# A hybrid encoder layer on one core: operands of the matmuls begin at many byte offsets in one block of each projection

## The chip, the cores and the metric

The kernel runs on one NeuronCore of a Trainium2 chip. The time is device microseconds of one execution. Of the kernel before, three timed runs gave 2269.83 to 2270.15 us, with a median of 2270.11 us. The core's engines are TensorE (matmuls, PE in the profile, its weight loads PEld), VectorE (DVE), ScalarE (ACT), GpSimd (POOL) and SyncE (SP), which here issues nearly all transfers. A matmul multiplies a stationary operand, which a weight load brings into the array first, with a moving operand that streams past it column by column.

## What is computed

One layer of an encoder over 2048 prompt tokens and 8 x 16 sample tokens, model width 1024. It has four large projections, and the change touches three of them:

```python
qm, km, vm, om, ip, fp, qa, ka, va = split_in(x @ w_in)      # input projection
...
mix = jnp.concatenate([hm, ha], axis=-1) @ w_out             # output projection
h = layer_norm(DEEPNORM_ALPHA * x + mix, ln1_g, ln1_b)
f, conv_rows = conv_ffn(h, conv_prev, w_up, w_conv, b_conv, w_down)
y = layer_norm(DEEPNORM_ALPHA * h + f, ln2_g, ln2_b)
...
u = h @ w_up                                                 # up-projection, 1024 -> 5632
c = b_conv + sum(ext[:, j:j + T] * w_conv[j] for j in range(CONV_W))
a, g = jnp.split(c, 2, axis=-1)
return (jax.nn.silu(g) * a) @ w_down                         # down-projection, 2816 -> 1024
```

Between the first two stand a matrix-memory head group and a sliding-window attention group, whose small matmuls are woven into the large ones.

## The kernel before

**Arithmetic.** Every operand of a large matmul is split into two fp32r parts, hi (a cast by ScalarE) and lo (what the cast left, a subtraction by VectorE); this is `split`, lines 220 to 223. A product is then three matmuls: hi x hi, hi x lo, lo x hi. Each projection uses seven products for a two by two block multiplication instead of eight (a Strassen-like scheme); s = 1 to 7 names the product, and some products take sums or differences of weight quadrants. Such sums are made once, in block 0, written to DRAM, and loaded in later blocks (`SUMS`).

**Weight slots.** Split weights lie in slots of `WS` = 1088 columns of fp32, of which a weight unit uses 1024, so that it can begin up to 64 columns (256 bytes) into the slot. Eight slots (tags wlo, whi) and two more (wex) are used in turn. `half` (line 399) gives a slot to the input and output projections, `f_slot` (line 1787) to the up- and down-projection; both take the column `at` at which the unit begins.

**Input projection.** Four blocks of tokens (`IBLOCKS`), in each five groups g of output columns and seven products s. `next_split` (line 474) takes the next weight unit: it is split on the chip, or, if `kept` (line 428: block over 0, g from 2 on, s one of 6, 5, 7, 3), both halves are loaded ready-made from DRAM. It begins at column 16 for g below 2 and at column 48 for g from 2 on. `i_product` (line 714, matmuls at line 726) runs 24 matmuls of 256 columns for a product; for g below 2 the weights are the stationary operand and the tokens move, from g = 2 on it is the other way round. `i_direct` (line 740, matmuls at line 752) multiplies the gate and key-value weights with 264 columns.

**Up-projection.** Three blocks of tokens (`FBLOCKS`: 6, 6 and 5 tiles of 128), 22 column pairs j in each, seven products for each pair. `f_next` (line 1806) makes the weights of the next product, up to 6 products ahead of the matmuls in block 0 and 8 ahead after it: in block 0 all are split on the chip, and those of `SUMS` are also written to DRAM; in blocks 1 and 2 those of `SUMS` are loaded and three (s = 1, 2, 4) are split. They begin at column 48. `f_tokens` (line 1764) splits a quarter of a block's tokens into tiles of 4 x 384 columns, of which it uses the first h, 384 in blocks 0 and 1 and 320 in block 2. In `f_product` (line 1894, matmuls at line 1902) the weights are stationary and the tokens move, 12 matmuls for a product.

**Down-projection.** The same three blocks, seven products in six units of depth. `d_weights` (line 2036) loads and splits the weights of a unit into two slots, beginning at column 0; they are the moving operand, 512 columns, at line 2112. `d_tokens` (line 2054) splits the tokens, which are stationary.

In all three, TensorE runs its instructions in the order in which the program lists them; loads are issued by SyncE in order; the casts and subtractions stand in the orders of ScalarE and VectorE.

Other instructions that the working names: line 1366 transposes the attention's probabilities out of a tile whose rows are 2 x 128 + 4 = 260 columns apart; lines 1235, 1237 and 1244 multiply by v and by the memory C, whose heads are 129 columns apart, in plain fp32; line 1247 updates C head by head; line 1960 is two of the three taps of the causal convolution, which read `u[:, 1:]` and `u[:, 0:]`; line 1116 loads v (`v` in the rows) into heads 129 columns apart.

Of the kernel before, what the change touches and what calls it, by code (L numbers as in the profile page):

```python
# [206 lines left out]
class Prog:  # L207
# [265 lines left out]
    def next_split(self):  # L473
        V = self.nc.vector
        if self.us >= self.ur:
            return False
        u = self.uq[self.us]
        need = 1 if u[0] == "g" else 2
        if self.halves[0] - self.halves[1] + need > self.ring:
            return False  # L480
        self.us += 1
        if u[0] == "g":
            e = self.raw_of.pop(u)
            w = self.half(0, WS).rearrange("p (i k m) -> p i k m", i=2, k=2)[:, :, :, :264]
            self.split(w[:, 0], w[:, 1], e[0])
            e[1] = True
            self.wu[u] = w[:, 0], w[:, 1]
            return True
        at = 0 if u[0] == "o" else 16 if u[2] < 2 else 48
        hi, lo = self.half(at, 1024), self.half(at, 1024)  # L490
        if self.kept(u):
            for i, t in enumerate((hi, lo)):
                self.nc.sync.dma_start(t.bitcast(F32), self.zws[u[2]][SUMS.index(u[3])][i].rearrange("p a b -> p (a b)"))
        elif u[0] == "p" and u[1] == 0:
            self.split_first(u[2], u[3], hi, lo)
        else:
            e = self.raw_of.pop(u)
            self.split(hi, lo, e[0].rearrange("p a b -> p (a b)"))
            e[1] = True
        v = lambda t: t.rearrange("p (a b) -> p a b", a=2 if u[0] == "o" else 4)  # L500
        self.wu[u] = v(hi), v(lo)
        return True
# [491 lines left out]
    def one(self, n, sh, dt=F32):  # L994
        return self.tp.tile(sh, dt, name=n, tag=n, bufs=1)
# [698 lines left out]
    def f_setup(self):  # L1694
        nc, a, fp = self.nc, self.a, self.fp
        one = lambda n, sh, dt=F32: fp.tile(sh, dt, name=n, tag=n, bufs=1)
        self.cw = one("cw", [P, NUP, 4])
        nc.sync.dma_start(self.cw, a["cw"])

        nc.vector.tensor_scalar_mul(self.cw[:, :NFF], self.cw[:, :NFF], 0.5)  # L1700
        self.prev = one("prev", [P, 2, NFF, 2])
        nc.vector.memset(self.prev, 0.0)
        self.hraw, self.hc, self.wr, self.wc = {}, {}, {}, {}
        self.slot, self.made, self.u2 = -1, 0, {}
        nb = len(FBLOCKS)

        pairs = [(b, j) for b in range(nb) for j in range(NFF)]
        self.seq = [(0, 0, 1), (0, 0, 7)]
        for g in range(len(pairs)):
            self.seq += [(*pairs[g + d], s) for d, s in ORDER if 0 <= g + d < len(pairs)]  # L1710

        self.seq[-3:] = [(nb - 1, NFF - 1, s) for s in (5, 2, 3, 4)]
# [51 lines left out]
    def f_tokens(self, b, *steps):  # L1764

        V = self.nc.vector
        R, W = self.hraw[b], len(FBLOCKS[b]) * P
        h = W // 2
        r1, r2, r3, r4 = R[:, :4, :h], R[:, :4, h:W], R[:, 4:, :h], R[:, 4:, h:W]
        src = {1: r1, 7: r2, 6: r2, 2: r3, 5: r1, 3: r4, 4: r3}  # L1770
        for s in steps:
            if s == "t1":
                V.tensor_sub(r1, r2, r1)
            elif s == "t3":
                V.tensor_sub(r2, r4, r2)
            elif s == "t2":
                V.tensor_sub(r2, r4, r1)
            elif s == "t4":
                V.tensor_sub(r3, r3, r2)
            else:  # L1780
                pool = self.fp if s in (1, 7, 6) else self.f3 if s == 4 else self.f2
                hi = pool.tile([P, 4, 384], F32R, name=f"hh{s}", tag=f"hh{s}", bufs=1)
                lo = pool.tile([P, 4, 384], F32R, name=f"hl{s}", tag=f"hl{s}", bufs=1)
                self.split(hi[:, :, :h], lo[:, :, :h], src[s])
                self.hc[b, s] = hi[:, :, :h], lo[:, :, :h]

    def f_slot(self, at, dt=F32R):
        self.slot = (self.slot + 1) % 10
        if self.slot < 8:
            w = self.wp.tile([P, WS], dt, name="uw", tag=("whi", "wlo")[self.slot % 2], bufs=WB)  # L1790
        else:
            w = self.wx.tile([P, WS], dt, name="uw", tag="wex", bufs=2)
        return w[:, at:at + D].rearrange("p (k m) -> p k m", k=KD)

    def f_raw(self, b, j):

        nc = self.nc
        v, g = [self.wp.tile([P, KD, P], F32, name=n, tag="wraw", bufs=WR) for n in ("wv", "wg")]
        nc.sync.dma_start(v, self.a["wup"][j])
        if b == 0:  # L1800
            nc.sync.dma_start(g, self.a["wup"][NFF + j])
        else:
            nc.sync.dma_start(g[:, 4:], self.a["wup"][NFF + j][:, 4:])
        self.wr[b, j] = v, g

    def f_next(self):

        nc, V = self.nc, self.nc.vector
        if self.made >= len(self.seq):
            return False  # L1810
        b, j, s = self.seq[self.made]
        self.made += 1
        if s == 1:
            if (b, j) not in self.wr:
                self.f_raw(b, j)
            if b == 0:
                v, g = self.wr[b, j]
                s12, s34 = self.f_slot(48, F32), self.f_slot(48, F32)
                V.tensor_add(s12[:, :4], g[:, :4], g[:, 4:])
                V.tensor_sub(s34[:, :4], v[:, :4], g[:, :4])  # L1820
                V.tensor_sub(s12[:, 4:], s12[:, :4], v[:, :4])
                V.tensor_sub(s34[:, 4:], v[:, 4:], s12[:, 4:])
                self.wr[b, j] = v, g, s12, s34
        if s == 5 and (b, j) != (len(FBLOCKS) - 1, NFF - 1):
            self.f_raw(b + (j + 1) // NFF, (j + 1) % NFF)
        w = self.f_slot(48).rearrange("p (i k) m -> p i k m", i=2)
        i = SUMS.index(s) if s in SUMS else None
        keep = None if i is None else self.zw[j][i].rearrange("p (i k m) -> p i k m", i=2, k=4)
        if b and i is not None:
            nc.sync.dma_start(w.bitcast(F32), keep)  # L1830
        else:
            r = self.wr[b, j]
            q = {1: lambda: r[0][:, :4], 2: lambda: r[0][:, 4:], 4: lambda: r[1][:, 4:], 5: lambda: r[2][:, :4],
                 6: lambda: r[2][:, 4:], 7: lambda: r[3][:, :4], 3: lambda: r[3][:, 4:]}[s]()
            self.split(w[:, 0], w[:, 1], q)
            if i is not None:
                nc.sync.dma_start(keep, w.bitcast(F32))
        self.wc[b, j, s] = w[:, 0], w[:, 1]
        return True
# [196 lines left out]
    def d_weights(self):  # L2036

        if self.nw >= len(self.dseq):
            return
        b, s, u = self.dseq[self.nw]  # L2040
        self.nw += 1
        ks = DUNITS[u]
        m, k0, c0 = {1: (None, 0, 0), 2: (None, NK2, 0), 3: (None, NK2, 512), 5: (0, 0, 0), 7: (0, 0, 512), 4: (1, 0, 0), 6: (1, 0, 512)}[s]
        src = self.a["wdn"] if m is None else self.zt[m]
        src = src[k0 + ks[0]:k0 + ks[-1] + 1, :, c0:c0 + 512].rearrange("k p n -> p k n")
        n = len(ks) * 512
        raw = self.wp.tile([P, 1024], F32, name="wraw", tag="wraw", bufs=WR)
        hi, lo = [self.f_slot(0).rearrange("p a b -> p (a b)") for _ in range(2)]
        v = lambda t: t[:, :n].rearrange("p (a b) -> p a b", b=512)
        self.nc.sync.dma_start(v(raw), src)  # L2050
        self.low = self.split(hi[:, :n], lo[:, :n], raw[:, :n])
        self.dw[b, s, u] = v(hi), v(lo)
# [183 lines left out]
```

## Time and profile before

| | |
|---|---|
| median of 3 runs | 2270.11 us (2269.83 to 2270.15) |
| the profiled execution | 2270.08 us, span 2268.3 us |
| TensorE busy | 2251.2 us, 14293 matmuls |
| weight loads busy | 2081.9 us |
| VectorE, ScalarE busy | 1807.6 and 1273.1 us |
| transfers | 631.30 MB, mean 278 GB/s |

The profile is one execution. Its page gives busy times of the engines, the chain of work that ended last, and groups of instructions by line of the kernel. The trace behind it also answers by stretches of time (busy time and count of each engine), by line (least, median and greatest duration) and in the order of time. A matmul's duration in a row is the time from its start to its modelled end, so matmuls in a row overlap; their pace is read from starts, or from a stretch and its count.

### The profile page before, as it was taken

Reading aid. Unit: us, or ns where it says so; the run is one execution under the profiler, and the core shown is the slowest. Engines: PE = TensorE matmul, PEld = TensorE weight load, DVE = VectorE, ACT = ScalarE, POOL = GpSimd, SP = SyncE. Lnnn points to the kernel's source line nnn. Section 1 sums busy time; section 2 is a strip of 40 time slices with the busy share of each in tenths; the row PEclk is TensorE's granted clock in tenths of the full one; section 3 lists DMA queues with packets and bytes.
Section 4 is the critical chain, followed back from the end, with each engine's and each line's share of the span. In section 5 each row is a group of like instructions: output and inputs, shape, how many; then the busy total and the mean of one; then the engine's idle time right before and its main releaser. Section 6 shows DMA issues by size and latency. Waiting matters only on the chain.

```text
span 2268.3 us, 39783 instructions
## 1 busy us (share of the span) xinstructions
PE 2251.2 (99%) x14293; PEld 2081.9 (92%) x14293; DVE 1807.6 (80%) x3069; ACT 1273.1 (56%) x2374; POOL 270.3 (12%) x509
## 2 busy tenths in 40 slices
PE   9999999999999999999999999999999999999998
PEld 8999999999878778999999999999999988888887
DVE  9787687777698888998778777678766787896997
ACT  5453476776776656555656555556555644444452
POOL 0001001000021110211112000003211200100100
PEclk9999999999999999999999999999999999999999
DMA  8888998898997767898777999988998796757752
GB/s 304 315 314 317 317 320 275 277 315 294 331 325 262 275 216 282 305 330 302 279 284 261 308 307 311 314 274 277 316 304 263 253 318 207 255 188 234 247 171 89
DMA packets 302277, 631.30 MB, mean 278 GB/s; under 512 B 47420, under 2 KB 140672, under 8 KB 302080
## 3 DMA queue, kind: packets, MB, share of 16 engines
q1 hardware_dynamic: 296832, 614.01, 78.9%
q0 software_dynamic: 3520, 10.56, 1.5%
q10 hardware_dynamic: 1728, 4.20, 0.5%
q8 instruction: 113, 1.85, 0.3%
q14 instruction: 84, 0.69, 0.1%
HBM read 457.02 MB, written 171.64 MB: 277 GB/s over the span
## 4 chain that ended last, share of the span: by engine, by line
PE 80%; DVE 5%; issue 1%; ACT 1%; DMA 1%; POOL 0%; DVEq 0%; SPq 0%; ACTq 0%; POOLq 0%
PE dps L1902 20%; PE fup L1902 20%; PE dps L726 8%; PE fup L2112 7%; PE dps L2112 7%; PE fht L2112 5%; PE dps L227 2%; PE dps L228 2%; PE dps L229 2%; PE ppo L1372 1%; PE dps L752 1%; PE psc L1327 1%; PE ppt L1366 1%; DVE w L223 1%; PE fht L1724 1%
## 5 line engine op out<-in xcount | busy, mean ns | idle before, releaser
L1902 PE MATMUL fup<-hh,uw 128*128 128x384 f32 (+1 forms) x1848 | 476.8, 327 | 0.0
L1902 PE MATMUL dps<-hh,uw 128*128 128x384 f32 (+1 forms) x1848 | 476.7, 327 | 0.0
L1902 PEld LDWEIGHTS fup<-hh,uw 128*128 128x128 f32 x1848 | 329.6, 188 | 0.1
L1902 PEld LDWEIGHTS dps<-hh,uw 128*128 128x128 f32 x1848 | 329.5, 188 | 0.0
L1902 PE MATMUL fup<-hl,uw 128*128 128x384 f32 (+1 forms) x924 | 301.9, 327 | 1.2 <-DVE hl L223 1.2
L1902 PE MATMUL dps<-hl,uw 128*128 128x384 f32 (+1 forms) x924 | 301.7, 327 | 0.0
L1960 DVE SCALAR_TENSOR_TENSOR cc<-u,cw,cc 128x768 f32<-128x768 f32 (+1 forms) x264 | 258.1, 978 | 38.5 <-ACT cc L1958 32.1
L726 PE MATMUL dps<-w,oh 128*128 128x256 f32 x1344 | 251.2, 283 | 0.2 <-ACT dps L820 0.2
L222 ACT CAST uw<-wraw 128x1024 fp32r<-128x1024 f32 x126 | 123.9, 983 | 216.1 <-PE dps L2112 117.9
L223 DVE TENSOR_TENSOR w<-wraw,w 128x1024 fp32r<-128x1024 f32 (+2 forms) x163 | 186.5, 1150 | 63.8 <-ACT w L222 61.7
L222 ACT CAST w<-wraw 128x1024 fp32r<-128x1024 f32 (+2 forms) x163 | 160.7, 992 | 110.8 <-PE dps L726 55.4
L726 PEld LDWEIGHTS dps<-w,oh 128*128 128x128 f32 x1344 | 209.7, 188 | 11.3 <-issue 8.1
L726 PE MATMUL dps<-w,ol 128*128 128x256 f32 x672 | 187.1, 278 | 0.0
L223 DVE TENSOR_TENSOR uw<-wraw,uw 128x1024 fp32r<-128x1024 f32 x126 | 142.3, 1129 | 53.8 <-ACT uw L222 53.7
L1902 PEld LDWEIGHTS fup<-hl,uw 128*128 128x128 f32 x924 | 173.6, 188 | 1.9 <-DVE hl L223 1.8
L1902 PEld LDWEIGHTS dps<-hl,uw 128*128 128x128 f32 x924 | 173.6, 188 | 0.0
L726 PE MATMUL dps<-oh,w 128*128 128x256 f32 x896 | 167.4, 283 | 2.0 <-ACT mr L1177 0.9
L2112 PE MATMUL fup<-uw,fu 128*128 128x512 f32 x726 | 168.9, 389 | 0.0
L2112 PEld LDWEIGHTS fup<-uw,fu 128*128 128x128 f32 x726 | 136.3, 188 | 28.3
L2112 PE MATMUL dps<-uw,fu 128*128 128x512 f32 x660 | 160.7, 389 | 0.0
L2112 PEld LDWEIGHTS dps<-uw,fu 128*128 128x128 f32 x660 | 123.9, 188 | 25.8
L726 PEld LDWEIGHTS dps<-oh,w 128*128 128x128 f32 x896 | 139.8, 188 | 7.9 <-issue 4.1
(319 smaller groups left out, 4555.8 us busy)
## 6 DMA issues: line engine op xcount, KB each, us to landing
uw<-zw SPq DMA_DIRECT2D x176, 512.0 KB, 5.1
zw<-uw SPq DMA_DIRECT2D x88, 512.0 KB, 3.4
w<-zws SPq DMA_DIRECT2D x72, 512.0 KB, 5.9
wv<-wup SPq DMA_DIRECT2D x66, 512.0 KB, 5.3
wraw<-wi SPq DMA_DIRECT2D x65, 512.0 KB, 5.3
wraw<-zt SPq DMA_DIRECT2D x60, 512.0 KB, 3.8
wraw<-wdn SPq DMA_DIRECT2D x45, 512.0 KB, 3.9
wraw<-wo SPq DMA_DIRECT2D x40, 512.0 KB, 4.4
```

Source lines behind the costliest of these rows:

```text
L222: nc.scalar.copy(hi, src)
L223: return nc.vector.tensor_sub(lo, src, hi.bitcast(F32)).ins
L227: mm(out, ah, bh, start=start, stop=False)
L228: mm(out, ah, bl, start=False, stop=False)
L229: mm(out, al, bh, start=False, stop=stop)
L726: mm(o, l, r, start=s in (1, 7) and c == k == i == 0, stop=k == 3 and i == 2, skip_group_check=True)
L752: mm(o, x, w, start=k == i == 0, stop=k == KD - 1 and i == 2, skip_group_check=True)
L1327: nc.tensor.matmul(ps[kvh][:, j, :nk], q[rs, j0 + j], k[rs, sel], start=i == 0, stop=i == 2)
L1366: nc.tensor.transpose(pp[:, j * P:(j + 1) * P], scs[j // 2][:, 2 * kvh + j % 2, kt * P:(kt + 1) * P], self.ident)
L1902: mm(ps, l[:, k], r[:, k], start=s in (1, 7) and k == 0 and i == 0, stop=k == 3 and i == 2, skip_group_check=True)
L1960: V.scalar_tensor_tensor(c[:, v], u[:, i:i + n], w[i], c[:, v], op0=ALU.mult, op1=ALU.add)
L2112: mm(ps, l[:, k, c], r[:, k], start=s in (1, 4, 7) and u == 0 and k == 0 and i == 0, stop=u == nu - 1 and k == n - 1 and i == 2, skip_grou ...
```

## The change

In one block of each of the three projections the weight units begin at varying columns of their slots, and in block 2 of the up-projection the tokens begin at varying columns of their tiles. Columns are 4 bytes. Tiles and slots keep their sizes and places, and instructions keep their number and order.

- Input projection, block 1: a split unit begins at `2 * (13 * us % 32)`, that is at multiples of 8 bytes from 0 to 248; a loaded one at `4 * (5 * us % 16)`, multiples of 16 bytes from 0 to 240; `us` counts the units.
- Up-projection, block 1, and block 2 from j = 11 on: a split unit begins 27 columns further than the last, modulo 64 (steps of 4 bytes); a loaded one 20 columns further, modulo 64 (steps of 16 bytes). Elsewhere 48 as before.
- Up-projection, block 2: the tokens of product s begin at column 0, 1, 2, 4, 8, 12 or 16 for s = 1, 7, 6, 2, 5, 3, 4.
- Down-projection, block 1: both slots of a unit begin at `2 * (13 * nw % 32)`, multiples of 8 bytes; `nw` counts the units.

```diff
@@ next_split
         at = 0 if u[0] == "o" else 16 if u[2] < 2 else 48
+        if u[0] == "p" and u[1] == 1:
+            at = 4 * (5 * self.us % 16) if self.kept(u) else 2 * (13 * self.us % 32)
         hi, lo = self.half(at, 1024), self.half(at, 1024)
@@ f_setup
+        self.begins = [0, 0]
@@ f_tokens
-                self.split(hi[:, :, :h], lo[:, :, :h], src[s])
-                self.hc[b, s] = hi[:, :, :h], lo[:, :, :h]
+                at = {1: 0, 7: 1, 6: 2, 2: 4, 5: 8, 3: 12, 4: 16}[s] if b == 2 else 0
+                hi, lo = hi[:, :, at:at + h], lo[:, :, at:at + h]
+                self.split(hi, lo, src[s])
+                self.hc[b, s] = hi, lo
@@ new
+    def f_begin(self, b, j, i):
+
+        if b == 0 or b == 2 and j < 11:
+            return 48
+        if i is None:
+            self.begins[0] = (self.begins[0] + 27) % 64
+            return self.begins[0]
+        self.begins[1] = (self.begins[1] + 20) % 64
+        return self.begins[1]
@@ f_next
-        w = self.f_slot(48).rearrange("p (i k) m -> p i k m", i=2)
         i = SUMS.index(s) if s in SUMS else None
+        w = self.f_slot(self.f_begin(b, j, i)).rearrange("p (i k) m -> p i k m", i=2)
@@ d_weights
-        hi, lo = [self.f_slot(0).rearrange("p a b -> p (a b)") for _ in range(2)]
+        at = 2 * (13 * self.nw % 32) if b == 1 else 0
+        hi, lo = [self.f_slot(at).rearrange("p a b -> p (a b)") for _ in range(2)]
```

## The prediction

> **What bounds the kernel now.** I read the page first, then the waits of TensorE, then a table of busy time by stage, and last single groups of instructions.
>
> ```profile
> span 2268.3 us, 39783 instructions
> PE 2251.2 (99%) x14293; PEld 2081.9 (92%) x14293; DVE 1807.6 (80%) x3069; ACT 1273.1 (56%) x2374; POOL 270.3 (12%) x509
> PEclk9999999999999999999999999999999999999999
> DMA packets 302277, 631.30 MB, mean 278 GB/s; under 512 B 47420, under 2 KB 140672, under 8 KB 302080
> PE 80%; DVE 5%; issue 1%; ACT 1%; DMA 1%; POOL 0%; DVEq 0%; SPq 0%; ACTq 0%; POOLq 0%
> ```
>
> The waits of TensorE (who waited for whom, us in total, times, longest), its two largest:
>
> ```profile
> PE dps L337 <- DVE zero L332: 2.0, 1, 2.0
> PE ppt L1539 <- POOL v L1117: 1.4, 1, 1.4
> ```
>
> The reader is to see that TensorE is busy for 99% of the span, at the full granted clock, and makes up 80% of the chain that ended last; its waits for others are a few single ones. So the kernel's time is the number of matmuls times the pace of one, and the change, which removes and adds no instruction, can move the time in one of two ways: the pace of a matmul depends on where its operands start, or an engine or a transfer that feeds TensorE becomes so slow that TensorE waits.
>
> The stages that the change touches, cut at the first and last matmul of each block (columns: window, its length, busy time and instructions of each engine, granted clock, share of the DMA engines, GB/s): block 1 of the input projection, the up-projection's block 0, block 1 and two halves of block 2, and the down-projection's three blocks.
>
> ```profile
> 162.26:286.61 124.35, 122.98 (x1118) 117.04 (x1117) 86.62 (x168) 55.30 (x102) 15.30 (x14) 1.00 0.92 317
> 886.77:1213.42 326.65, 326.18 (x1898) 325.35 (x1897) 283.96 (x406) 194.70 (x325) 51.81 (x90) 1.00 0.80 295
> 1213.42:1538.54 325.12, 324.42 (x1889) 323.73 (x1889) 244.37 (x287) 175.86 (x275) 40.45 (x89) 1.00 0.89 296
> 1538.54:1674.72 136.18, 136.18 (x926) 136.17 (x925) 105.09 (x150) 73.52 (x138) 34.55 (x91) 1.00 0.92 310
> 1674.72:1810.40 135.68, 135.68 (x927) 135.68 (x926) 94.11 (x136) 75.45 (x141) 27.23 (x87) 1.00 0.84 262
> 1810.71:1967.99 157.28, 157.28 (x694) 129.91 (x693) 124.80 (x150) 72.61 (x90) 4.96 (x7) 1.00 0.76 262
> 1967.99:2125.26 157.27, 157.27 (x695) 129.92 (x694) 133.72 (x166) 71.35 (x87) 11.25 (x13) 1.00 0.66 218
> ```
>
> From these come the paces. The down-projection's block 1 has 693 matmuls of 512 columns (7 products, 11 slices of depth, 3 token groups, 3 terms): 157.27 / 693 = 226.9 ns. The second half of block 2 of the up-projection has 11 x 7 x 12 = 924 of 320 columns: 135.68 / 924 = 146.8 ns. The difference gives (226.9 - 146.8) / 192 = 0.417 ns a column, and 226.9 - 512 x 0.417 = 13.4 ns a matmul that doesn't depend on its width. At 384 columns that makes 173.5 ns. Block 1 of the up-projection (1848 of them) takes 325.12 / 1848 = 175.9 ns, its token transposes included.
>
> At 256 columns, in the input projection, two paces stand side by side in the order of time (start, length, instruction):
>
> ```profile
> 223.68 0.28 PE L726 MATMUL dps<-w,ol 128*128 128x256 f32 x1
> 226.51 0.28 PE L726 MATMUL dps<-w,ol 128*128 128x256 f32 x1
> 404.88 0.28 PE L726 MATMUL dps<-w,ol 128*128 128x256 f32 x1
> 405.90 0.28 PE L726 MATMUL dps<-w,ol 128*128 128x256 f32 x1
> 409.28 1.05 PE L1152 MATMUL pscore<-qk 128*128 128x128 f32 x8
> 410.17 0.60 PE L1162 MATMUL pkt<-ident,qk 128*128 128x128 f32 x4
> ```
>
> Between the first two rows lie 24 matmuls, 2.83 / 24 = 118 ns; between the next two lie 9, 1.02 / 9 = 113 ns. Eight passes of 128 columns took 0.89 us, 111 ns each, and each had its own weight load; so a weight load of 128 columns takes at most 111 ns. It is covered by 2 to 7 ns at 256 columns, by 36 ns at 320, by 62 ns at 384 and by 116 ns at 512.
>
> **The change part by part.** Where the starts move, counted from the code:
>
> - Input projection, block 1: 35 weight pairs. 23 are split on the chip (starts in steps of 8 bytes), 12 are loaded (steps of 16). For g below 2 the weights are stationary (14 products, 336 matmuls); for g from 2 on they are the moving operand (9 split and 12 loaded products, 216 and 288 matmuls).
> - Up-projection, block 1 and block 2 from j = 11: 99 split weight pairs in steps of 4 bytes (792 + 396 matmuls), 132 loaded ones in steps of 16 bytes. Weights are stationary here.
> - Up-projection, block 2: tokens, the moving operand, 264 matmuls for each product; s = 7, 6, 2, 5, 3, 4 start 4, 8, 16, 32, 48 and 64 bytes in, s = 1 stays.
> - Down-projection, block 1: 42 weight pairs, the moving operand of 693 matmuls, steps of 8 bytes.
>
> No instruction, tile or queue order changes: the last start is 62 of 64 spare columns in a weight slot, and 16 + 320 of 384 in a token tile.
>
> *Casts and subtractions.* They now write and read at starts off 8 and 16 bytes. What the trace has of that:
>
> ```profile
> L1960 DVE SCALAR_TENSOR_TENSOR cc<-u,cw,cc x87: 1009/1019/1022, 1221.4 to 1535.1; 128x768 f32<-128x768 f32 x87
> L1247 DVE SCALAR_TENSOR_TENSOR C<-C,wi,pcu x64: 322/342/351, 319.4 to 828.7; 128x129 f32<-128x129 f32 x64
> ```
>
> Columns are minimum, median and maximum in ns. Every second instruction of line 1960 reads at an odd word (u[:, 1:]), the others at an even one: all lie within 13 ns. Line 1247 reads and writes heads 129 words apart, so at all four words of 16 bytes: within 29 ns. I take 0 to 29 ns a split, and 0 for the time: VectorE is busy 244 of 325 us and 134 of 157 us in the stages concerned, behind TensorE's matmuls, and 42 splits of 29 ns are 1.2 us in the fuller one. Without that cover they would cost those 1.2 us there, 99 x 29 ns = 2.9 us in the up-projection and 0.7 us in the input projection. ScalarE (176 of 325 us) has more room.
>
> *Weight loads (stationary).* Nearest rows: the transposes of line 1366 take weights 260 words apart, so at all steps of 16 bytes within 64.
>
> ```profile
> L1366 PEld LDWEIGHTS ppt<-ident,sc x248: 137/141/144, 326.0 to 837.8; 128*128 128x128 f32 x124
> L1237 PE MATMUL pnum<-C,qk x120: 275/275/275, 348.7 to 827.0; 128*128 128x129 f32 x120
> L1244 PE MATMUL pcu<-v,kw x128: 272/275/277, 315.4 to 827.9; 128*128 128x129 f32 x128
> ```
>
> Within 7 ns: steps of 16 bytes are free. For 4 and 8 bytes there is no row; bounds are 0 and a load that takes twice as long (a rival below). A single extra piece of 16 bytes, 111 / 32 = 3.5 ns, vanishes behind 36 ns and more in the up-projection and costs at most 3.5 - 2 = 1.5 ns on half of 336 matmuls, 0.3 us. I take 0.3.
>
> *Moving operands.* Lines 1237 and 1244 stream operands that start at every word of 16 bytes (heads 129 words apart), and last the same to 5 ns. But these stream plain fp32, in two passes of half the rate (111 ns for 128 columns above, against 128 x 0.417 = 53); for fp32r at 0.417 ns a column every start in the trace is a multiple of 64 bytes. So the price is bounded: nothing from below; from above twice the column time. A stream read in pieces of 16 bytes, which is 4 columns, would cost one piece more for a start off 16 bytes: 1.67 ns. Such starts have 2 x 264 token matmuls, half of 693 and half of 216, together 983: 1.6 us. I take it, as the row nearest to this, the fp32 one, shows none or very little. Should the 13.4 ns between matmuls absorb it, the cost is nothing.
>
> [...]
>
> *Loads.* 24 transfers into the input weights and 132 into the up-projection's now land 16-byte steps off; issue, size and queue stay.
>
> ```profile
> uw<-zw SPq DMA_DIRECT2D x176, 512.0 KB, 5.1
> w<-zws SPq DMA_DIRECT2D x72, 512.0 KB, 5.9
> v<-zv SPq DMA_DIRECT2D x17, 256.0 KB, 6.5
> og<-zog SPq DMA_DIRECT2D x17, 256.0 KB, 5.5
> ```
>
> v lands in rows 516 bytes apart, so at starts of 4, 8 and 12 bytes, and takes 6.5 us against 5.5 for og: up to 18% longer, bounds 0 to 18%. The weights are asked for 8 products ahead, 8 x 12 x 147 ns = 14 us, so a landing 1 us later hides there. I take 0; without that lead each late landing would show as idle time of TensorE.
>
> **The sum.** The profiled execution took 2270.08 us (span 2268.3 and 1.8 around it), 0.03 from the median of 2270.11. 2270.1 + 0.3 + 1.6 = 2272.0 us; with the bounds of these terms alone 2270 to 2274.
>
> **The rivals.**
>
> *Larger pieces.* If the moving stream is read in pieces of 32 bytes, a start off them costs 8 x 0.417 = 3.3 ns. Such starts: 4 x 264 token matmuls, 3/4 of 693, 3/4 of 216 and half of 288, 1882 in all: 6.3 us, 2276.4. With pieces of 64 bytes it is 6.7 ns on 5 x 264 + 7/8 x 693 + 7/8 x 216 + 3/4 x 288 = 2331: 15.5 us, 2285.6. Against 64 bytes speaks the matmul of 264 columns, 16.5 pieces:
>
> ```profile
> 286.61 11.65 PE dps L752 x96
> ```
>
> 11.65 / 96 = 121.4 ns; 17 full pieces would be 272 x 0.417 + 13.4 = 126.8 ns. 32 bytes remain open. Chance 0.20, slower.
>
> *Halved rate.* If an operand off its granule costs two reads for each piece over its whole length, it decides from the first such start. Odd words alone: 264 matmuls of s = 7 gain 320 x 0.417 = 133 ns, 35 us; odd weight loads last 222 ns, 49 over the 173 ns of 396 matmuls and 75 over the 147 ns of 198, 34 us: 2339. With 16 bytes as the granule: 528 x 133 + 347 x 213 + 108 x 107 ns = 156 us, and loads 594 x 49 + 297 x 75 + 168 x 107 = 69 us: 2495. For it: full rate is not shown off 64 bytes. Against it: the fp32 rows above and VectorE's line 1960, where a contiguous stream shows nothing. Chance 0.14.
>
> *Transfers become the bound.* In block 1 of the up-projection the 88 loads are 46 of 96 MB, so 0.43 of the share of 0.89. From packets about a quarter longer the DMA engines are full and TensorE waits; twice as long gives 325 x 0.32 = 104 us there, by the same reckoning 52 in block 2 and 27 in the input projection: 2453. The 18% of v falls short of it. Chance 0.06. [...]
>
> *Faster.* If the two paces at 256 columns come from the starts, block 1's 840 matmuls could all fall to 113 ns: 840 x 4.6 = 3.9 us, 2266.2; more only if the 13.4 ns shrink as well. Against: both paces above come from products with the same start, 192 bytes past a multiple of 256. Chance 0.08, most of it counted as faster.
>
> **How the numbers follow.** Forecast 0.50, within 0.2% (4.5 us, about what a measurement of this kernel can tell from no change); remaining 0.02 for slower. Faster 0.07, same 0.51, slower 0.42. The range goes from 2266 (the faster rival) to 2290 (the larger pieces with some 4 us of late feeding) and leaves out 0.2 for the halved rate and the transfers.
>
> **What would show it.** The same windows: the down-projection's block 1 against block 0 (157.27 and 157.28 us now) shows the moving weights, block 2's halves (136.18 and 135.68) the tokens and, in the second, the weights; block 1 of the up-projection the stationary ones alone. A step of more than 2 us in one of them names the rival. A DMA share near 1.00 with idle TensorE names the transfers. If VectorE's splits grow by over 100 ns, the first step is wrong. The prediction fails if any window of these grows by over 1%.

## The result and the profile after

Five timed runs of the changed kernel gave 2278.86 to 2281.33 us, median 2279.27; five of the kernel before 2269.83 to 2270.73, median 2270.15. The ratio is 1.0043, with a 95% interval of 1.0028 to 1.0057: slower by 9.1 us. The profiled execution took 2281.05 us, 10.97 more than the profiled one before.

The page of the changed kernel, the lines that answer to those shown of before:

```profile
span 2279.3 us, 39783 instructions
PE 2260.4 (99%) x14293; PEld 2086.9 (92%) x14293; DVE 1808.0 (79%) x3069; ACT 1273.5 (56%) x2374; POOL 277.0 (12%) x509
PEclk9999999999999999999999999999999999999999
uw<-zw SPq DMA_DIRECT2D x176, 512.0 KB, 4.9
```

TensorE has the same 14293 matmuls at the same clock and is still busy for 99% of the span, but busy 9.2 us longer (2260.4 against 2251.2). So nearly all of the time went into matmuls, not into waiting for something else. The loads of the up-projection's kept weights take no longer (4.9 us against 5.1). VectorE's total is the same to 0.4 us, and the two convolution taps, now line 1975, again take at most 1022 ns.

Busy time by stage, cut at the matmuls at which the table of before is cut: block 1 of the input projection, block 1 and the two halves of block 2 of the up-projection, blocks 0 and 1 of the down-projection.

```profile
162.28:287.88 125.60, 124.22 (x1118) 118.26 (x1117) 86.81 (x168) 55.23 (x102) 14.93 (x14) 1.00 0.93 314
...
1215.13:1543.05 327.92, 327.24 (x1889) 326.57 (x1889) 244.49 (x287) 176.47 (x275) 40.40 (x89) 1.00 0.90 294
1543.05:1680.93 137.88, 137.12 (x926) 136.85 (x925) 105.09 (x150) 73.80 (x138) 33.60 (x91) 1.00 0.91 306
1680.93:1817.31 136.38, 136.38 (x927) 136.38 (x926) 94.29 (x136) 75.73 (x141) 27.34 (x88) 1.00 0.86 260
1817.60:1974.92 157.32, 157.32 (x695) 129.95 (x693) 124.31 (x149) 72.75 (x90) 6.75 (x5) 1.00 0.77 261
1974.92:2136.20 161.28, 161.28 (x694) 130.42 (x693) 134.59 (x167) 71.11 (x87) 15.52 (x13) 1.00 0.66 214
```

Against before, the stages grew by 1.25, 2.80, 1.70, 0.70, 0.04 and 4.01 us, 10.5 of the 10.97; the rest lies ahead of the up-projection, in stretches that differ by up to 2.3 us between kernels that have the same starts there (598.9 to 601.2 us, at the last experiment below). Each stage that the change touches grew; block 0 of the down-projection, which it doesn't touch, kept its time. The biggest item is block 1 of the down-projection: 4.01 us on 693 matmuls is 5.8 ns each. In the first half of block 2, 0.76 of the 1.70 us are idle time of TensorE: its list of waits has a single one of 0.8 us there, of line 1917 for ScalarE's line 1946. This wait isn't the change's doing: two experiments below that leave the up-projection alone, `down_pieces` and `down_tokens`, have it too (0.3 and 0.8 us).

What exactly became longer is seen in the groups of instructions of the down-projection's block 1: the matmuls and their weight loads before, in their own fence, then the same after. The last number but the idle time is the mean of one in ns.

```profile
L2112 PE MATMUL fup<-uw,fu 128*128 128x512 f32 x265 | 62.3, 389 | 0.0
L2112 PEld LDWEIGHTS fup<-uw,fu 128*128 128x128 f32 x265 | 49.7, 188 | 10.3
```

```profile
L2128 PE MATMUL fup<-uw,fu 128*128 128x512 f32 x264 | 63.7, 395 | 0.0
L2128 PEld LDWEIGHTS fup<-uw,fu 128*128 128x128 f32 x264 | 49.7, 188 | 11.8
```

The matmuls last 395 ns instead of 389, as their starts lie 5.8 ns further apart; the weight loads are recorded with 188 ns, as before. That figure alone proves little, since the loads of the up-projection are recorded with 187 to 188 ns too, where in block 2 a new matmul with its load starts every 147 ns. What speaks for a slower stream, and against a load that has become the longer of the two, are the widths below: where a start costs something, a matmul takes about 233 ns at 512 columns, 177 to 178 at 384 and 149 at 320. A load that set the pace would give the same figure at each width.

By start, this block suggests that the price doesn't follow how round the start is. Four units of 18 matmuls, whose weights begin 72, 32, 0 and 112 bytes into their slots:

```profile
1983.33:1987.57 4.24, 4.24 (x20) 3.40 (x18) 4.24 (x8) 1.78 (x2) 2.57 (x2) 1.00 0.85 300
2010.59:2014.79 4.20, 4.20 (x20) 3.37 (x18) 4.20 (x6) 1.82 (x3) 0.00 (x0) 1.00 0.51 153
...
2056.70:2060.79 4.09, 4.09 (x19) 3.38 (x18) 2.10 (x2) 1.78 (x2) 0.00 (x0) 1.00 1.03 342
2079.71:2083.79 4.08, 4.08 (x20) 3.38 (x18) 2.09 (x2) 1.78 (x2) 0.00 (x0) 1.00 0.57 172
```

Divided by 18, a matmul takes 235.6, 233.3, 227.2 and 226.7 ns. The multiple of 32 bytes costs nearly as much as the start at 72, and 112 bytes, no multiple of 32, costs nothing here. But 112 bytes aren't free by themselves: the same unit, with the same starts and after the same unit at 8 bytes, takes 4.15 / 18 = 230.6 ns a matmul in `only_down`, the first experiment below.

```profile
2071.66:2075.81 4.15, 4.15 (x19) 3.38 (x18) 2.10 (x2) 1.79 (x2) 0.00 (x0) 1.00 0.45 131
```

One start can thus settle at two paces, which limits what any single stretch below can prove.

### The profile page after: what moved, and what is told of

Same layout as the page of the kernel before. It is cut to its first block, busy times and chain, and to the rows that moved or that the text cites. A ratio compares the mean times of both kernels' runs of the same rounds, so it can differ in the third digit from the quotient of the medians.

```text
span 2279.3 us, 39783 instructions
## 1 busy us (share of the span) xinstructions
PE 2260.4 (99%) x14293; PEld 2086.9 (92%) x14293; DVE 1808.0 (79%) x3069; ACT 1273.5 (56%) x2374; POOL 277.0 (12%) x509
## 4 chain that ended last, share of the span: by engine, by line
PE 78%; DVE 6%; DMA 2%; ACT 2%; issue 1%; POOL 0%; SPq 0%; DVEq 0%; ACTq 0%; POOLq 0%
PE dps L1917 20%; PE fup L1917 20%; PE fup L2128 7%; PE dps L728 7%; PE dps L2128 7%; PE fht L2128 5%; PE dps L227 2%; PE dps L229 2%; PE dps L228 2%; DVE w L223 1%; PE ppo L1374 1%; PE psc L1329 1%; PE ppt L1368 1%; PE fht L1727 1%; PE dps L754 1%
```

## The experiments

Four theories are weighed in what follows. **Own start**: each stream is read in pieces of a fixed size, its granule, and a start off them costs something for each matmul, as the prediction had it. **Variation**: what costs is that the start changes from unit to unit. **Distance**: two streams run side by side, the moving operand and the next matmul's weights (in the down-projection's block 1 above, loads are recorded for 130.42 of the 161.28 us, in which matmuls are busy throughout), and what counts is how their two starts lie to each other. **Feeding**: late loads or splits. The trace above already spoke against the last.

### The parts add up: only_down, without_down

`only_down` has the change in the down-projection alone; `without_down` has all the rest of it.

```diff
# only_down: before, with
-        hi, lo = [self.f_slot(0)...
+        at = 2 * (13 * self.nw % 32) if b == 1 else 0
+        hi, lo = [self.f_slot(at)...
# without_down: the changed kernel, with these lines undone
```

> The down-projection's part of the change alone: weights of block 1 begin at multiples of 8 bytes. If the parts add, 2270.1 + 4.0 = 2274.2 us (the 693 matmuls of that block took 161.28 us in the changed kernel and 157.27 before), and all other stages as before. If the parts disturb each other through the feeding of TensorE, less than that here.

> The change without its down-projection part. If the parts add: 2269.8 + 1.3 (input projection) + 2.8 (up-projection, block 1) + 1.4 (block 2) = 2275.3 us, so that this and the down-projection alone (4.5 us over before) make 10.0, against 9.1 measured for all. If the feeding of TensorE decides, the parts do not add, and stray waits show in the list of TensorE's waits.

`only_down`: 2274.31 us against 2269.82 beside it, ratio 1.0020 (1.0011 to 1.0029). `without_down`: 2275.36 against 2270.25, ratio 1.0024 (1.0015 to 1.0034). 4.5 + 5.1 = 9.6 us, and the whole change costs 9.1: within these intervals the parts add. By stage, `only_down` (the input projection's block 1, and the down-projection's block 1):

```profile
162.01:285.79 123.78, 122.41 (x1118) 116.46 (x1117) 86.75 (x168) 55.36 (x102) 15.33 (x14) 1.00 0.94 321
...
1966.89:2128.20 161.31, 161.31 (x694) 130.42 (x693) 134.57 (x167) 71.17 (x87) 15.53 (x13) 1.00 0.65 213
```

`without_down` (the up-projection's block 1 and the two halves of block 2):

```profile
1214.10:1542.02 327.92, 327.24 (x1890) 326.58 (x1889) 244.45 (x287) 176.31 (x275) 40.24 (x89) 1.00 0.88 293
1542.02:1678.88 136.86, 136.86 (x927) 136.86 (x925) 105.37 (x150) 74.65 (x138) 34.08 (x91) 1.00 0.93 308
1678.88:1815.25 136.37, 136.37 (x927) 136.37 (x926) 94.28 (x136) 75.70 (x141) 27.26 (x88) 1.00 0.85 260
```

Block 1 of the down-projection costs the same 4.0 us alone, block 1 of the up-projection the same 2.80. Without the single wait the first half of block 2 grows by 0.68 us: this is the price of the moved tokens. One caution comes from the first row: the input projection's block 1 takes 123.78 us here with the starts of before, where the profile of before has 124.35. Seven of the profiles have that block unchanged; four take the longer time and three the shorter. Differences of half a microsecond in that block mean nothing, and its growth is 1.25 us or 1.8, by which of the two one compares with.

### A fixed start: up_const

Block 1 and 2 of the up-projection; weights (stationary) at a start that stays the same for five column pairs: 148, 160, 212, 216 and 192 bytes.

```diff
-        w = self.f_slot(48)...
+        at = (37, 40, 53, 54, 48)[min(j // 5, 4)] if b else 48
+        w = self.f_slot(at)...
```

> Kernel before, but in blocks 1 and 2 of the up-projection the weights begin at one fixed byte offset for five column pairs j each: 148 (j 0 to 4), 160 (5 to 9), 212 (10 to 14), 216 (15 to 19), then 192 as before. The tokens stay. Five j are 420 matmuls, 72.8 us at the 173.3 ns of 384 columns. Theory 'own start' (a weight load costs more when it begins off a multiple of 4, 8 or 16 bytes): 160 is the cheapest, like before; 148 and 212 (odd words) the dearest, 216 between. Theory 'distance' (the load of the next weights and the moving stream disturb each other, and the distance of their starts decides, aligned or not), with the single products of the changed kernel as its numbers: 148 and 216 like before (173.3 ns, 72.8 us), 160 about 178 ns (74.7 us), 212 about 179.7 ns (75.5 us). Theory 'variation' (only a start that differs from the unit before costs): all four like before.

2276.8 us. Stretches of 30 products that lie wholly within one start; first before (block 1 twice, the second stretch with 16 other matmuls in it, then block 2), then `up_const` (148, 160, 212 and 216 bytes in block 1, then the same four in block 2):

```profile
1220.64:1283.04 62.40, 62.40 (x362) 62.40 (x362) 49.30 (x59) 32.50 (x51) 7.08 (x20) 1.00 0.88 292
1366.24:1430.43 64.19, 64.19 (x378) 64.01 (x378) 46.74 (x57) 34.73 (x56) 5.55 (x18) 1.00 0.94 314
1667.68:1720.48 52.80, 52.80 (x362) 52.80 (x361) 35.68 (x53) 27.07 (x51) 8.30 (x34) 1.00 0.88 275
```

```profile
1221.40:1285.00 63.60, 63.60 (x362) 63.60 (x361) 49.28 (x59) 32.57 (x51) 7.11 (x20) 1.00 0.86 289
1295.61:1359.21 63.60, 63.60 (x361) 63.60 (x361) 46.67 (x57) 32.94 (x52) 5.63 (x18) 1.00 0.90 303
1369.93:1436.02 66.09, 66.09 (x378) 65.89 (x378) 46.64 (x57) 34.93 (x56) 5.70 (x18) 1.00 0.91 307
1447.45:1511.69 64.24, 64.24 (x378) 64.11 (x378) 46.62 (x56) 34.79 (x56) 5.91 (x18) 1.00 0.90 305
1550.25:1603.05 52.80, 52.80 (x361) 52.80 (x361) 42.35 (x60) 28.93 (x53) 14.77 (x37) 1.00 0.93 310
1611.85:1664.65 52.80, 52.80 (x363) 52.80 (x361) 39.59 (x58) 27.27 (x53) 9.60 (x34) 1.00 0.95 322
1673.51:1727.08 53.57, 53.57 (x362) 53.57 (x361) 35.80 (x53) 27.18 (x51) 8.30 (x34) 1.00 0.87 270
1735.84:1788.30 52.46, 52.46 (x362) 52.46 (x361) 35.66 (x53) 27.00 (x51) 8.30 (x34) 1.00 0.88 272
```

In block 1 (384 columns) 148 and 160 bytes both cost 1.20 us on 360 matmuls, 3.3 ns each; 212 bytes 1.90 on 376, 5.1 ns; 216 bytes nothing. In block 2 (320 columns) 148 and 160 cost nothing, 212 costs 0.77 / 360 = 2.1 ns, 216 gains 0.9 ns. So variation is out: a start that doesn't vary costs as well. A granule for the stationary operand's own start is out as well: an odd word (148) and a multiple of 32 bytes (160) cost the same in block 1 and 216 bytes nothing, and the same starts of 148 and 160 cost 3.3 ns in one block and nothing in the next. The two blocks differ in the width of the matmul and in what ran before; which of the two decides isn't shown.

### The moving operand, alone and with the stationary one: down_const, down_both

In the down-projection's block 0 the weights (moving) get one start for each product; in block 2, where each of the products s = 4, 6 and 7 has tokens of its own, the tokens (stationary) move along by the same distance, but for s = 7 of `down_const`, where the weights move alone.

```diff
# down_const (down_both has other numbers), d_weights and d_tokens
+        at = {0: {1: 28, 2: 18, 4: 30, 6: 16, 5: 32, 3: 48, 7: 1}, 2: {4: 18, 6: 30, 7: 18}}.get(b, {}).get(s, 0)
-        hi, lo = [self.f_slot(0)...
+        hi, lo = [self.f_slot(at)...
...
+        if b == 2 and s in (4, 6):
+            at = {4: 18, 6: 30}[s]
+            w = w[:, :, :, at:at + h]
# down_both
+        at = {0: {1: 64, 2: 4, 4: 8, 6: 2, 5: 60, 3: 56, 7: 44}, 2: {4: 16, 6: 8, 7: 4}}.get(b, {}).get(s, 0)
...
+        if b == 2 and s in (4, 6, 7):
+            at = {4: 16, 6: 8, 7: 4}[s]
+            w = w[:, :, :, at:at + h]
```

> Kernel before, but in the down-projection the weights of a whole product (99 matmuls of 512 columns, 22.4 us at 226.7 ns) begin at one fixed byte offset. Block 0, in the order of the products: s = 1: 112, 2: 72, 4: 120, 6: 64, 5: 128, 3: 192, 7: 4. Block 2 (66 matmuls for the products named): s = 4: weights and tokens both 72 bytes in, s = 6: both 120 in, s = 7: weights alone 72 in. Block 1 as before. 'Own start': 64, 128 and 192 are free (22.4 us), 112 too if 16 bytes are the granule, 72 and 120 cost about 0.7 to 0.8 us each, 4 at least as much; in block 2 both operands off 16 bytes cost at least as much a matmul as the weights alone. 'Distance': 112 free, 64 about +0.3 us, 128 about +0.5, 192 about +0.6, 72 +0.85, 120 +0.74, 4 unknown; in block 2 s = 4 and s = 6 are free (226.7 ns) and s = 7 costs 8 ns a matmul, 0.5 us. 'Variation': nothing costs, since the start stays through a product.

> Down-projection again, all else as before. Block 2, weights and tokens moved by the same amount: s = 4 by 64 bytes, s = 6 by 32, s = 7 by 16 (66 matmuls each, 226.7 ns before). Block 0, the weights alone, 99 matmuls each: s = 1: 256 bytes, 2: 16, 4: 32, 6: 8, 5: 240, 3: 224, 7: 176. Both streams at 72 and at 120 bytes cost 4.9 and 7.4 ns a matmul, the weights alone at 64 cost 6.6, so neither the distance alone nor the alignment alone tells the price. Theory 'distance in whole lines' (the two reads meet in the same part of the memory, which is laid out in lines; a common move by whole lines changes nothing): all common moves by at least one line are free, so 64 free if lines have at most 64 bytes, 32 too if at most 32, 16 too if at most 16; 72 and 120 aren't whole lines of 16. Theory 'own place' (each start counts for itself, modulo 256): common moves cost like the weights alone, 6.6 ns at 64. In block 0, by both theories 256 is free; by 'distance' the others cost 4 to 9 ns, aligned or not, and 16 and 32 no less than 8.

Before, a product of 99 matmuls in block 0, and 64 matmuls of a product in block 2:

```profile
1810.71:1833.15 22.44, 22.44 (x100) 18.58 (x99) 16.62 (x20) 11.02 (x15) 0.01 (x1) 1.00 0.91 288
2170.14:2184.64 14.50, 14.50 (x65) 12.01 (x64) 14.50 (x23) 7.41 (x10) 0.00 (x0) 1.00 0.44 133
```

`down_const`, 2275.05 us: weights alone at 112, 72, 64 and 4 bytes (99 matmuls), both operands at 72 and at 120, weights alone at 72 (64 matmuls):

```profile
1809.50:1832.38 22.88, 22.88 (x100) 18.56 (x99) 16.67 (x20) 11.06 (x15) 0.01 (x1) 1.00 0.91 297
1832.38:1855.67 23.29, 23.29 (x100) 18.70 (x99) 20.84 (x24) 11.33 (x16) 0.00 (x0) 1.00 1.02 394
1878.80:1901.90 23.10, 23.10 (x101) 18.71 (x99) 15.97 (x20) 9.98 (x12) 0.00 (x0) 1.00 0.66 219
...
1948.01:1971.52 23.51, 23.51 (x101) 18.72 (x100) 23.04 (x33) 10.04 (x13) 7.32 (x6) 1.00 0.76 264
2173.69:2188.51 14.82, 14.82 (x65) 12.11 (x64) 14.82 (x23) 7.42 (x10) 0.00 (x0) 1.00 0.41 128
2188.98:2203.96 14.98, 14.98 (x65) 12.08 (x64) 14.78 (x24) 10.40 (x18) 0.00 (x0) 1.00 0.69 221
2227.32:2242.39 15.07, 15.07 (x65) 12.08 (x64) 11.31 (x14) 8.82 (x11) 0.00 (x0) 1.00 0.16 52
```

`down_both`, 2273.06 us: weights alone at 256, 16 and 32 bytes (99 matmuls), both operands at 64, 32 and 16 (64 matmuls):

```profile
1809.11:1831.56 22.45, 22.45 (x100) 18.59 (x99) 16.64 (x20) 11.03 (x15) 0.02 (x1) 1.00 0.88 291
1831.56:1854.49 22.93, 22.93 (x100) 18.61 (x99) 20.57 (x24) 11.66 (x16) 0.00 (x0) 1.00 1.05 405
1854.49:1877.58 23.09, 23.09 (x101) 18.56 (x99) 22.72 (x28) 9.96 (x12) 0.00 (x0) 1.00 0.55 179
...
2172.41:2186.96 14.55, 14.55 (x66) 12.01 (x64) 14.55 (x23) 7.41 (x10) 0.00 (x0) 1.00 0.40 130
2187.42:2201.95 14.53, 14.53 (x65) 12.01 (x64) 14.53 (x23) 10.54 (x17) 0.00 (x0) 1.00 0.68 221
2225.72:2240.45 14.73, 14.73 (x66) 11.99 (x65) 11.31 (x14) 8.80 (x11) 0.00 (x0) 1.00 0.16 53
```

The pair that decides is 32 bytes: weights alone there take 23.09 / 99 = 233.2 ns a matmul, 6.6 more than at 0; with the tokens moved by 32 bytes too, 14.53 / 64 = 227.0, as good as free. The same with 64: alone 23.10 / 99 = 233.3, together 14.55 / 64 = 227.3. A start by itself is neither good nor bad; how the two streams lie to each other is what counts. Weights alone at 256 bytes are free again (226.8). At all the other starts that these two runs gave to the weights alone, round or not, the matmuls take longer, from 231.1 ns at 112 bytes to 237.5 at 4.

But the distance isn't all: moved together by 16, 72 and 120 bytes, matmuls take 230.2, 231.6 and 234.1 ns, 3.5 to 7.4 more, although the distance stays. All three are no multiples of 32. At 72 bytes the common move is still cheaper than that of the weights alone (231.6 against 15.07 / 64 = 235.5).

### How far it goes: down_pieces, down_tokens

`down_pieces` moves both operands in block 2, by 96, 48 and 8 bytes. `down_tokens` moves the tokens alone, by 192, 64 and 256 bytes.

```diff
# down_pieces, d_weights and d_tokens
+        at = {(2, 4): 24, (2, 6): 12, (2, 7): 2}.get((b, s), 0)
...
+        if b == 2 and s in (4, 6, 7):
+            at = {4: 24, 6: 12, 7: 2}[s]
+            w = w[:, :, :, at:at + h]
# down_tokens, d_tokens alone
+        if b == 2 and s in (4, 6, 7):
+            at = {4: 48, 6: 16, 7: 64}[s]
+            w = w[:, :, :, at:at + h]
```

> Block 2 of the down-projection, both operands moved by the same distance: 96 bytes (s = 4), 48 bytes (s = 6), 8 bytes (s = 7); 66 matmuls of 512 columns for each of the three products, 226.7 ns each before. Pieces of 32 bytes: 96 is free (under 0.8 ns), 48 and 8 cost 3 to 8 ns a matmul, 2270.5 to 2271.2 us in all. Pieces of 16 bytes: 96 and 48 are free, only 8 costs. The distance alone: all three are free. Every start that is no multiple of 64 bytes costs: 96 costs as well, 3 ns or more.

> Block 2 of the down-projection, the tokens (stationary) alone moved: 192 bytes (s = 4), 64 bytes (s = 6), 256 bytes (s = 7); the weights (moving) stay. If the distance of the two starts modulo 256 bytes decides, tokens at 192 stand as weights at 64 did (233.3 ns a matmul in block 0) and tokens at 64 as weights at 192 (233.4 ns), both 231 to 235 ns, and 256 is free (226.7): 2271 us in all. If only the moving operand's own start has a price, all three are free, 226.7 ns and 2270.2 us. If the order of the two matters, 192 and 64 differ by over 2 ns.

`down_pieces`, 2270.53 us (2271.28 beside it), 64 matmuls of each of the three products:

```profile
2169.80:2184.35 14.55, 14.55 (x66) 12.01 (x64) 14.55 (x23) 7.39 (x10) 0.00 (x0) 1.00 0.45 139
2184.81:2199.73 14.92, 14.92 (x65) 12.03 (x64) 14.71 (x24) 10.32 (x18) 0.00 (x0) 1.00 0.69 207
2223.08:2237.90 14.82, 14.82 (x65) 12.10 (x64) 11.29 (x14) 8.79 (x11) 0.00 (x0) 1.00 0.15 53
```

96 bytes: 227.3 ns, free. 48: 233.1, 8: 231.6. So a common move is free at 32, 64 and 96 bytes and costs at 8, 16, 48, 72 and 120: pieces of 32 bytes fit all eight, pieces of 16 fail on 16 and 48. Each of the eight is one stretch of one run.

`down_tokens`, 2271.82 us:

```profile
2171.35:2185.99 14.64, 14.64 (x65) 12.02 (x64) 14.56 (x23) 7.41 (x10) 0.00 (x0) 1.00 0.48 144
2186.45:2201.39 14.94, 14.94 (x66) 12.03 (x65) 14.72 (x24) 10.32 (x18) 0.00 (x0) 1.00 0.65 203
2224.73:2239.24 14.51, 14.51 (x65) 12.01 (x64) 11.29 (x14) 8.79 (x11) 0.00 (x0) 1.00 0.16 54
```

Tokens alone at 64 bytes take 233.4 ns and at 256 nothing extra (226.7), as the distance has it: moving the stationary operand slows the stream just as moving the streamed one does. Yet 192 bytes take 228.8, where 231 to 235 was expected because weights at 64 took 233.3. A distance taken modulo 256 bytes is therefore too simple to give the price. Whether the two directions differ, or this is another case of one relation that settles at two paces, one stretch doesn't tell.

### Can starts be chosen to gain: in_const, starts_chosen

In the input projection `in_const` gives each block one start for stationary and one for moving weights; `starts_chosen` then takes those that looked best, and 216 bytes in the up-projection's block 2.

```diff
# in_const
+        if u[0] == "p":
+            at = ((12, 16), (22, 28), (56, 8), (0, 40))[u[1]][u[2] > 1]
# starts_chosen
-        at = 0 if u[0] == "o" else 16 if u[2] < 2 else 48
+        at = 0 if u[0] == "o" else 22 if u[2] < 2 else 28
...
-        w = self.f_slot(48)...
+        w = self.f_slot(54 if b == 2 else 48)...
```

> Kernel before, but in the input projection the weights begin at one fixed byte offset in each block (g below 2, where they are stationary; g from 2 on, where they move): block 0: 48 and 64, block 1: 88 and 112, block 2: 224 and 32, block 3: 0 and 160 (before: 64 and 192 everywhere). It asks whether the two paces of 256 columns, 113 and 118 ns, follow the distance of the two starts. 'Distance': whole blocks sit at one pace, and 88 (113.5 ns in one product of the changed kernel) and 112 (115 to 117) are the fast ones; the best case for block 1 is 3 us less than before. 'Own start': 64, 32, 160, 0 and 224 alike, 88 slower. If the paces come from interruptions by other matmuls, all blocks show both, as before, and the time stays within 2 us of 2270.

> A version with starts chosen from these traces: input projection at 88 bytes for g below 2 and 112 for g from 2 on in every block (block 1 of the run with fixed starts had 75 and 81% of its matmuls at the fast pace, against 37 and 21% before), up-projection block 2 at 216 bytes (145.7 ns against 146.7 there). If the two paces follow the starts: 336 x 1.8 + 504 x 2.6 ns in block 1, about half of that each in blocks 2 and 3, so 3.7 us, and 1848 x 1.0 ns = 1.8 us: 5.5 us below the kernel before, about 2264.4. If the paces of the input projection come from interruptions: only the 1.8 us, 2268.

`in_const` took 2272.3 us. Its block 1 (starts at 88 and 112 bytes), and all that follows up to the up-projection (blocks 2 and 3 with 224, 32, 0 and 160 bytes):

```profile
162.72:285.50 122.78, 121.08 (x1118) 115.16 (x1117) 86.41 (x168) 55.23 (x102) 15.32 (x14) 1.00 0.94 324
285.46:887.95 602.49, 600.64 (x4253) 520.23 (x4251) 477.27 (x1232) 409.48 (x1010) 76.61 (x103) 1.00 0.85 288
```

The second stretch takes 600.20 us before (286.57 to 886.77), so these blocks seemed to lose 2.3 us, while block 1 seemed to gain 1.0 to 1.6. But kernels that leave the input projection alone take from 598.9 (`down_both`) to 601.2 us (`down_tokens`) for the second stretch, so the loss is 1.3 to 3.6 us by the kernel one compares with, and whether the two paces of 256 columns follow the starts stays open. `starts_chosen` was to turn that into a gain: 2268.96 us against 2270.25, ratio 0.9995 (0.9986 to 1.0004), which can't be told from no change. The input projection's block 1 took 123.11 us against 123.78 and 124.35 with the old starts, and the second half of the up-projection's block 2 this:

```profile
1673.81:1809.50 135.69, 135.69 (x927) 135.69 (x926) 94.14 (x136) 75.56 (x141) 27.34 (x87) 1.00 0.84 262
```

That is 135.68 before: the 0.9 ns a matmul that 216 bytes had gained there in `up_const` didn't come again. The expectation of 2264.4 failed; the 2268 of its other theory is met only in number, since the 1.8 us on which it rested, from 216 bytes, aren't there. With that went the hope that a table of good starts can be read from one run.

## Why the prediction was right or wrong

The direction was right and the time lay inside the range, but the forecast of 2272.0 was 7.3 us short: the sum gave the change 1.9 us, and it costs 9.1. The forecast of "within 0.2%" failed with it, and so did the prediction by its own sign: no window was to grow by over 1%, and the down-projection's block 1 grew by 2.5%. That the time lies in the range is luck, for its upper end came from 32-byte pieces priced stream by stream and from 4 us of late feeding, and neither is what happened.

- **What bounds the kernel** held. TensorE's busy time grew by 9.2 us, and the stages of the tables carry the whole difference: 1.25 + 2.80 + 0.68 + 0.70 + 4.01 = 9.4 us.
- **Casts and subtractions at no cost** held: VectorE's total is 1808.0 us against 1807.6.
- **Loads at no cost** held: 4.9 us to landing against 5.1 in the up-projection, DMA share 0.90 against 0.89 in its block 1, and no wait of TensorE for a load in its list. The input projection's loads took 6.3 us against 5.9, inside the bound of 18% and without a wait.
- **Weight loads (stationary), 0.3 us**: this step failed. In the up-projection's block 1 they are the only thing moved, and it grew by 2.80 us. The prediction took the danger to be a longer load, and hid it behind 36 ns of cover. The recorded loads didn't get longer (188 ns); the matmuls streaming beside them did. Cover for the load says nothing about that. `down_tokens` shows it alone: with only the stationary operand moved 64 bytes, a matmul takes 233.4 ns instead of 226.7, at 512 columns, where the prediction saw 116 ns of cover.
- **Moving operands, 1.6 us**: the term was mis-sized, and the step behind it (a start off 16 bytes costs one piece more) was wrong. Half of the down-projection's 693 matmuls were to pay 1.67 ns each, 0.6 us; the block grew by 4.01. Unit by unit in the changed kernel, all starts but 0, 112 and 64 bytes pay 3.9 ns or more, multiples of 16 among them, and 64 pays 3.1. The tokens' share came out close to its term by another road: 0.68 us in the first half of block 2, where the prediction had 0.44 (264 starts off 16 bytes). No run shows pieces of 16 bytes, from which this term and the 0.3 us were built: moved together by 16 and 48 bytes the operands cost 3.5 and 6.4 ns a matmul at 512 columns (`down_both`, `down_pieces`). The fp32 rows on which the small price rested show no effect of their starts (272 to 277 ns for 129 columns); the fp32r matmuls do (395 ns against 389 in the down-projection's block 1). (The last start in a weight slot is column 63, reached in the up-projection, and not 62; it still fits, and nothing hangs on it.)
- **The rivals.** The larger pieces saw something: 32 bytes is a size that the runs show (common moves of 32, 64 and 96 bytes took 227.0 to 227.3 ns a matmul). But the rival priced each stream by its own start, 3.3 ns off a piece and nothing on it, and weights alone at 32 bytes cost 6.6 ns. Its 2276.4 us is nearer to the result than the forecast, by a reckoning that isn't the one at work. The halved rate is out (no start cost more than 11 ns a matmul), the transfers too (DMA share 0.90 in the up-projection's block 1, no wait for a load). The faster one needed starts that help: `starts_chosen` looked for them and found no gain that can be measured.

What the prediction lacked is a rival in which two streams that are each fine alone disturb each other. The evidence within reach was that in the kernel before every pair of fp32r streams starts at multiples of 64 bytes, so that its rows could show neither the common nor the single move.

**What stays open.** That two reads at the same time share some part of the memory is argued from the pace, which depends on both starts (233.2 ns for weights alone at 32 bytes, 227.0 for both operands there), and from the unchanged record of the loads (188 ns); it is not shown, and a matmul without a weight load beside it was not tried. The rule for the price isn't known either. It may depend on the direction (228.8 and 233.4 ns for tokens at 192 and 64 bytes) and on the width (3.3 ns at 384 columns, none at 320 for 160 bytes). And the starts alone don't fix it: weights at 112 bytes took 226.7 ns a matmul in the changed kernel, 230.6 in the same unit of `only_down`, where even the unit before was the same, and 22.88 / 99 = 231.1 in `down_const`. So something besides the starts of a unit and of the unit before it decides, and what it is isn't known. The prediction had met the like in the input projection, where matmuls of 256 columns ran at 118 and at 113 ns with one start.

## What to carry to other kernels

Where TensorE is the bound and streams as here (fp32r, with a weight load for each matmul, 226.7 ns for 512 columns), keep the two starts of a matmul in the relation that a fast stage already has; a move of one operand by 256 bytes left the pace as it was (226.8 ns for the weights, 226.7 for the tokens). When a tile must be moved otherwise, move both operands by the same multiple of 32 bytes: that was free three times out of three here (227.0 to 227.3 ns at 32, 64 and 96 bytes), each time in one stretch of one run, while one operand alone, even at 32 or 64 bytes, cost some 3% of each matmul (233.2 to 233.4 ns). When pricing such an edit, don't stop at "the weight load has cover": ask what streams while it runs. And read a start's price in the stage in which it will run, more than once, since the same start cost 3.3 ns in one block and nothing in the next, and a gain of 0.9 ns in one run didn't come again.

## What was not expected of the hardware

Moving the stationary operand alone, whose load had 116 ns to spare by the prediction's estimate, by 64 bytes lengthened the matmuls (from 226.7 to 233.4 ns between starts) and left the recorded loads at 188 ns. A move by 64 bytes cost 6.6 ns for one operand and 0.6 for both. One and the same start settled at two paces, 226.7 and 230.6 ns at 512 columns, in the same unit of two runs. Next to that, the starts had no price for the splits: in the up-projection's block 1 a subtraction of 512 columns on VectorE took 693 ns at steps of 4 bytes, against 692 before, and a cast on ScalarE 622 against 621.
